# Transpositions of activations, norms and attention operands issued one at a time between split products instead of in runs

## The chip, the cores and the metric

The kernel runs on one core of one Trainium2 chip. The metric is device time in microseconds (us), the median of several executions. One execution is also profiled; its trace gives the start and the duration of every instruction on each engine: PE (TensorE, matmuls and transpositions), PEld (its weight loads), DVE (VectorE), ACT (ScalarE), POOL (GpSimd) and SP (SyncE, which here issues the DMAs). Each engine takes its own instructions in the order in which the program holds them.

## The reference

256 tokens of 1024 features pass through two blocks; every number is float32.

```python
def reference(x, ...):
    x = first_block(x, ...)    # h = rmsnorm(x); x += short_conv_mixer(h)   h = rmsnorm(x); x += swiglu(h)
                               # h = rmsnorm(x); x += mla_mixer(h)          h = rmsnorm(x); x += moe_swiglu(h)
    return second_block(x, mem_2, ...)

def mla_mixer(h, ...):         # 8 heads; queries and keys of 128 + 64 (rope) features
    down = h @ w_down
    c_q, c_kv = rmsnorm(down[..., :384]), rmsnorm(down[..., 384:640])
    q, kv = c_q @ w_uq, c_kv @ w_ukv
    q, k = rmsnorm(q), rmsnorm(k)          # then rope on 64 of the 192 features
    p = softmax(mask(q @ k.T * scale));  return (p @ v) @ w_o

def moe_swiglu(h, router, w_gate, w_up, w_down):   # 8 experts, the best two of each token
    gates = top_k(softmax(h @ router), 2)
    for e in range(8): out += gates[:, e] * swiglu(h, w_gate[e], w_up[e], w_down[e])

def second_block(x, mem, ...):
    z = rmsnorm(h) @ w_in                          # q, k, v of 8 heads of 64, pooling input, forget logits
    fox = forgetting_attention(q, k, v, f_logit)   # causal softmax with a decay
    pool = multiscale_pool(p_in, w_pool, pool_scale)   # trailing means of 4 groups, a linear map, a scale
    h += concat(fox, pool) @ w_out
    h += attention_to(mem) @ w_mem_out
    h += swiglu(rmsnorm(h))
```

## The kernel before

All work is in one program, written as steps. A string such as `MLA_ORDER` lists the steps of a stage; `play` appends them, and `run` calls them one after the other. The order in which steps are called is the order of the instructions in every engine's queue; nothing reorders them later. A step `f1` or `f2` only converts one or two more pieces of weights.

Products are **split products**: a float32 operand is held as a rounded high part (a cast on ACT) and the rest as a low part (a subtraction on DVE, `split_to`, L219 and L220), and `mm3` issues three matmuls, high by high, low by high, high by low (L225 to L227). Weights arrive by DMA as `raw`, are cast to `wh` on ACT and reduced to `wl` on DVE, some 1.0 and 1.2 us for each piece of 128x1024, all through the kernel. The matmuls of a product have 512, 384, 320 or 256 columns.

A **transposition** is a matmul with the identity (`ident`) of a 128x128 block. A helper issues a run of 2 to 4 of them into one bank of PSUM with the tag `t`, and then at once the instruction that empties the bank: a split (ACT cast, DVE subtraction) for norms and activations, a copy on ACT or DVE for attention operands. There are **two** banks of that tag, taken in turn; outputs of attention values, pooling products (`pooled`, `mapped`) and the experts' gather take them too. So a transposition or a product that opens such a bank waits until the last but one has been emptied.

Where transpositions stand: `Norm.turn(t)` (line L710 of `transposed`) transposes the rows of one of the two token tiles t after a norm, 8 of them, for the next stage; steps `zt` (t = 0) and `w` (t = 1). `Experts.turn` (L1236) transposes an expert's activations, 16 for each expert in four runs of four. In MLA, `turn` (L664) has the steps `R`, `K`, `Q` (rope part, key, query of a pair of heads, 4 each; R and K are emptied on ACT, Q on DVE, L666), and `causal_turn` (L552, step `y`) the three blocks of a softmax. In the forgetting attention (FOX) `turn` (L916) has `Q` (emptied on DVE) and `K` (on ACT, L918). In both, `s` are score products (L508, L509), `v` value products (L559, L560), `k` and `q` the products of keys and queries, `zp` products of the output projection, and in FOX `g` and `x` the pooling's two products; an `x` is scaled on ACT (L908) and split. After the last `zp` of a stage, the residual is added on DVE (L361), squared on ACT (L1147) and normed on DVE (L1160).

Of the kernel before, what the change touches and what calls it, by code (L numbers as in the profile page):

```python
# [68 lines left out]
FFN_HEAD = ("f1 f2 a00 f2 f1 a10 f2 f1 w a20 f1 f2 a21 a01 a30 f2 a31 f2 a11 f1 f2 f2 f2 f1 f1 f2 A u04 f2 f2 f2 "  # L69
    "f1 T f2 u05 f1 f1 f1 o0 o1 f2 f2 f2 f2 o2 f1 f2 f2 u06 f1 f2 u07 f1 f2 f1 f2 f1")  # L70
FFN_TAIL = ("f1 zp000 f2 zp010 zp001 zp011 zr00 zs00 f2 zp100 zr01 zs01 zp101 f2 zn0 zr10 f2 zp110 f1 zs10 zp111 "
    "zr11 zt zs11 zn1")
MLA_ORDER = ("b00 B a00 f2 w f2 p a10 a01 b01 c0 f2 f1 a11 f2 b10 c1 L0 b11 h0 L1 f2 h1 k00 l0 k01 f2 k10 l1 f2 "
# [5 lines left out]
ROUTE_ORDER = ("k00 f1 n0 w k01 r0 n1 k10 r1 R k11 K O S f2 f1 G0 f1 f2 G1 f1 B f2")  # L79
TAIL_ORDER = ("v00 d00 d01 d10 d20 d11 h0 d21 f2 c00 h1 c10 v01 c11 zs10 f1 f2 f2 f2 zs00 zs11 c01 zs01 zn0 f1 zn1 "  # L80
    "v10 f2 zt f2 f2 f2 f1 v11 V f2")
FOX_ORDER = ("w b a000 a010 S00 a001 a100 F0 f1 f2 U00 a011 S01 F1 a101 f2 U01 D a111 S11 a110 a201 a200 S10 a210 "
# [7 lines left out]
FFN2_HEAD = ("f2 f2 a00 a10 f2 f1 f2 w a20 f2 f1 a01 a21 a11 a30 a31 f1 f1 A f2 u04 f1 f2 f1 T f2 f2 u05 f2 f2 f1 "  # L90
# [3 lines left out]
class Chunk:  # L94
    """A chunk of weights in DRAM, and once it is on chip, its two float32r parts."""
# [22 lines left out]
class Body:  # L118
    def __init__(self, ctx, tc, t, out):
# [8 lines left out]
        self.steps = []  # L128

# [4 lines left out]
    def add(self, fn, *chunks, rate=None):  # L134
        """rate: pieces of chunks ahead at the step's start."""
        for c in chunks:
            if c.first is None:
                c.first = len(self.steps)
            c.last = len(self.steps)
        self.steps.append((fn, chunks, AHEAD[1] if rate is None else rate))  # L140

    def run(self):
        order = list(dict.fromkeys(c for _, chunks, _ in self.steps for c in chunks))
        at = {c: i for i, c in enumerate(order)}
        self.loaded = done = need = 0  # chunks; pieces of chunks; chunks

        def piece():
            """The next piece of a chunk into its parts."""
# [12 lines left out]
        def fill(n):  # L161
            """Up to n pieces of chunks ahead."""
# [7 lines left out]
        for s, (fn, chunks, rate) in enumerate(self.steps):  # L170
# [31 lines left out]
    def buf(self, tag, shape, dt=F32):  # L202
        """A working tile; TAGS says how many of its kind there are."""
# [3 lines left out]
    def split(self, src):  # L207
        """Both parts of [128, 256] or [128, 512], in a tile each or in one."""
# [21 lines left out]
    def row(self, name, n, tag=None):  # L230
        """A row of the parameter vector, on every partition."""
# [5 lines left out]
    def rstd(self, tag, ss, n, width):  # L237
        """(ss / width + eps) ** -0.5 of a few columns."""
# [7 lines left out]
    def setup(self, gain):  # L246
# [10 lines left out]
        # TensorE's clock rises with use: it starts before the first rows are there  # L257
# [4 lines left out]
    def constants(self):  # L262
# [5 lines left out]
        # causal mask of a diagonal block: 0 where key <= query  # L268
# [4 lines left out]
        # triu[j, t] = 1 where j <= t; striu: j < t  # L273
# [12 lines left out]
        # 1 / (t + 1) of the first frames  # L286
# [3 lines left out]
        # the narrow weights of the router and of the forget gates: high and low parts side by side  # L290
# [7 lines left out]
    def rope_tables(self):  # L298
# [23 lines left out]
        def wrap(dst, src):  # L322
            # into [-pi, pi]
# [44 lines left out]
    def entering(self, norm):  # L368
        """Steps of a norm of the residual stream."""
        return norm and {"zs": lambda t, n: (lambda: norm.stats(t, n),), "zn": lambda t: (lambda: norm.scale(t),),  # L370
                         "zt": lambda: (lambda: norm.turn(0),), "w": lambda: (lambda: norm.turn(1),)} or {}

    def project(self, acc, c, r, part, start):
        """acc[t, n] += part.T @ row r of the chunk."""
# [48 lines left out]
    def ffn(self, norm, gu0, gu, down, nxt, orders):  # L423
        """gu0: gate and up of the first 512 features, by rows of tokens; gu: of the others, by features."""
# [6 lines left out]
        def row_part(i, t):  # L431
            """Chunk i % 2 of gate (i < 2) or up: k-tiles 4 (i % 2)... ."""
# [1048 lines left out]
```

## Time and profile before

| | |
|---|---|
| time, median of 3 executions | 1384.9 us (1384.81 to 1385.75) |
| span of the profiled execution, first to last instruction | 1383.6 us |
| mean granted TensorE clock over the span | 0.988 |
| PE busy | 1337.0 us, 97% of the span |
| DVE busy | 1012.6 us, 73% |
| ACT busy | 814.8 us, 59% |
| PE matmuls | 7395 |

The profiled execution has no time of its own apart from its span; the median stands 1.3 us above it, which is what lies around the first and last instruction. Busy shares are averages over stages. Matmuls are pipelined and overlap in the records, so starts, not durations, tell what a matmul costs: the distance from one start to the next.

### The profile page before, as it was taken

How to read it: one execution, taken by the hardware profiler on the slowest of the kernel's cores; microseconds unless marked ns; L12 is line 12 of the kernel's file. 1: busy time of each engine (PE TensorE's matmuls, PEld its weight loads, DVE VectorE, ACT ScalarE, POOL GpSimd, SP SyncE). 2: the span in 40 equal slices, each digit the busy share in tenths (PEclk: the TensorE clock that was granted, in tenths of full speed). 3: DMA queues.
4: the chain of work that ended last, by engine and by line, in shares of the span. 5: the costliest groups of instructions: out<-in, count | busy, mean ns of one | idle time of the engine just before them, and what ended most of it. 6: DMA issues, size and time to landing. Idle time of an engine off the chain costs nothing.

```text
span 1383.6 us, 18935 instructions
## 1 busy us (share of the span) xinstructions
PE 1337.0 (97%) x7395; PEld 1152.1 (83%) x7395; DVE 1012.6 (73%) x1346; ACT 814.8 (59%) x1198; POOL 35.3 (3%) x70
## 2 busy tenths in 40 slices
PE   7999999999997999999999999999989888999998
PEld 7997999987776888888888888888868777899997
DVE  5866465558777898998989898989976566654554
ACT  4544454446655786867777777777755455634442
POOL 1000000001000000000000000000002000000000
PEclk9999999999999999999999999999999899999999
DMA  7545455435334999898989898989963332444441
GB/s 274 216 183 187 163 213 183 175 114 199 131 117 175 342 351 351 335 355 340 352 326 364 322 370 321 365 321 359 353 257 127 116 118 107 159 176 182 183 183 61
DMA packets 49328, 329.54 MB, mean 238 GB/s; under 512 B 6352, under 2 KB 7248, under 8 KB 11216
## 3 DMA queue, kind: packets, MB, share of 16 engines
q1 hardware_dynamic: 48672, 328.18, 63.9%
q8 instruction: 59, 0.97, 0.3%
q14 instruction: 37, 0.30, 0.1%
q10 hardware_dynamic: 560, 0.09, 0.0%
HBM read 327.20 MB, written 1.05 MB: 237 GB/s over the span
## 4 chain that ended last, share of the span: by engine, by line
PE 64%; DVE 3%; ACT 1%; issue 0%; POOL 0%; DVEq 0%; ACTq 0%; POOLq 0%
PE ps L225 19%; PE ps L227 19%; PE ps L226 19%; PE ps L1200 2%; PE ps L1236 1%; DVE wl L220 1%; PE ps L1246 0%; PE ps L1245 0%; PE ps L508 0%; PE ps L559 0%; DVE e L893 0%; PE ps L710 0%; DVE n L1160 0%; PE ps L1065 0%; ACT wh L219 0%
## 5 line engine op out<-in xcount | busy, mean ns | idle before, releaser
L220 DVE TENSOR_TENSOR wl<-raw,wh 128x1024 fp32r<-128x1024 f32 (+2 forms) x622 | 717.3, 1201 | 97.9 <-ACT wh L219 96.2
L219 ACT CAST wh<-raw 128x1024 fp32r<-128x1024 f32 (+2 forms) x622 | 611.3, 1035 | 125.6 <-PE ps L226 87.5
L225 PE MATMUL ps<-x,wh 128*128 128x256 f32 x800 | 228.1, 285 | 0.3 <-ACT e L889 0.2
L227 PE MATMUL ps<-x,wh 128*128 128x256 f32 x800 | 227.4, 284 | 0.0
L226 PE MATMUL ps<-x,wl 128*128 128x256 f32 x800 | 227.4, 284 | 0.0
L225 PE MATMUL ps<-wh,n 128*128 128x512 f32 x560 | 222.4, 397 | 0.0
L227 PE MATMUL ps<-wl,n 128*128 128x512 f32 x560 | 218.6, 390 | 0.0
L226 PE MATMUL ps<-wh,n 128*128 128x512 f32 x560 | 218.1, 389 | 0.0
L225 PE MATMUL ps<-wh,x 128*128 128x512 f32 (+2 forms) x448 | 175.4, 392 | 0.3 <-ACT x L219 0.2
L227 PE MATMUL ps<-wl,x 128*128 128x512 f32 (+2 forms) x448 | 173.2, 387 | 1.8 <-DVE wl L220 1.8
L226 PE MATMUL ps<-wh,x 128*128 128x512 f32 (+2 forms) x448 | 172.6, 385 | 1.1 <-DVE x L220 1.1
L225 PEld LDWEIGHTS ps<-x,wh 128*128 128x128 f32 x800 | 154.1, 193 | 2.0 <-DVE c L220 0.5
L226 PEld LDWEIGHTS ps<-x,wl 128*128 128x128 f32 x800 | 154.2, 193 | 0.8
L227 PEld LDWEIGHTS ps<-x,wh 128*128 128x128 f32 x800 | 154.1, 193 | 0.2 <-DVE x L220 0.2
L227 PEld LDWEIGHTS ps<-wl,n 128*128 128x128 f32 x560 | 105.1, 188 | 23.0
L226 PEld LDWEIGHTS ps<-wh,n 128*128 128x128 f32 x560 | 105.3, 188 | 20.9
L225 PEld LDWEIGHTS ps<-wh,n 128*128 128x128 f32 x560 | 105.2, 188 | 20.6
L227 PEld LDWEIGHTS ps<-wl,x 128*128 128x128 f32 x448 | 84.1, 188 | 20.2 <-DVE wl L220 3.6
L467 ACT ACTIVATE e<-ps 128x256 f32<-128x256 f32 x36 | 13.9, 385 | 144.8 <-PE ps L227 144.8
L226 PEld LDWEIGHTS ps<-wh,x 128*128 128x128 f32 x448 | 84.2, 188 | 17.7 <-DVE x L220 2.1
L225 PEld LDWEIGHTS ps<-wh,x 128*128 128x128 f32 x448 | 84.2, 188 | 16.0 <-ACT x L219 0.7
L468 DVE TENSOR_TENSOR e<-e,ps 128x256 f32<-128x256 f32 x36 | 15.2, 421 | 101.5 <-ACT e L467 101.5
(302 smaller groups left out, 1443.2 us busy)
## 6 DMA issues: line engine op xcount, KB each, us to landing
raw<-in_moe SPq DMA_DIRECT2D x192, 1024.0 KB, 5.3
raw<-in_ffn_gu SPq DMA_DIRECT2D x22, 1024.0 KB, 4.9
raw<-in_gu SPq DMA_DIRECT2D x22, 1024.0 KB, 4.8
raw<-in_conv_in SPq DMA_DIRECT2D x11, 1024.0 KB, 5.8
raw<-in_ffn_down SPq DMA_DIRECT2D x11, 1024.0 KB, 4.9
raw<-in_down SPq DMA_DIRECT2D x11, 1024.0 KB, 4.9
raw<-in_w_mem SPq DMA_DIRECT2D x6, 1024.0 KB, 4.9
raw<-in_w_in SPq DMA_DIRECT2D x6, 1024.0 KB, 6.3
```

The source lines that it names most:

```text
L219: self.nc.scalar.copy(hi, src)
L220: self.nc.vector.tensor_tensor(lo, src, hi.bitcast(F32), ALU.subtract)
L225: mm(ps, lhsT=a[0], rhs=b[0], start=start, stop=False)
L226: mm(ps, lhsT=a[1], rhs=b[0], start=False, stop=False)
L227: mm(ps, lhsT=a[0], rhs=b[1], start=False, stop=stop)
L467: nc.scalar.activation(sg, b[:, :S], AF.Silu)
L468: nc.vector.tensor_mul(h, sg, b[:, S:])
L1200: nc.tensor.matmul(o, lhsT=self.norm.h[t][:, (k0 + k) * P:(k0 + k + 1) * P], rhs=sel[:, t], start=t == 0, stop=t == NT - 1)
L1236: nc.tensor.transpose(ps[:, k * P:(k + 1) * P], h[n][:, k * P:(k + 1) * P], b.ident)
```

## The change

Transpositions are no longer issued where their step stands. `turning` makes one function for each, the last of which also empties the bank; `between` puts them in a list; `mm3` takes one from the list after each of its three matmuls; and `run` issues what is left in a run at the end of a step that took any. Score and value steps of both attentions first issue what is waiting. The norm's steps have a second form, `wd` and `zd`, which put the transpositions in the list; `wd` replaces `w` in the two swiglu stages, MLA, the routing and FOX, and `zd` with a place one product step earlier replaces `zt` at the end of the first swiglu.

```diff
-FFN_HEAD = ("f1 f2 a00 f2 f1 a10 f2 f1 w a20 ...
+FFN_HEAD = ("f1 f2 a00 f2 f1 a10 f2 f1 wd a20 ...
...
-FFN_TAIL = (... "zn0 zr10 f2 zp110 f1 zs10 zp111 zr11 zt zs11 zn1")
+FFN_TAIL = (... "zn0 zr10 f2 zp110 f1 zs10 zd zp111 zr11 zs11 zn1")
...
-ROUTE_ORDER = ("k00 f1 n0 w k01 r0 n1 ...
+ROUTE_ORDER = ("k00 f1 n0 wd k01 r0 n1 ...
...
+            self.took = False
             fn()
+            if self.took:
+                self.flush()
...
+    def between(self, fns, now=False):
+        self.waiting += fns
+        if now:
+            self.flush()
+
+    def flush(self):
+        while self.waiting:
+            self.waiting.pop(0)()
+
+    def turning(self, srcs, after):
+        bank = []
+        def one(i, src):
+            if not bank:
+                bank.append(self.bank("t"))
+            m = src.shape[-1]
+            self.nc.tensor.transpose(bank[0][:m, i * P:(i + 1) * P], src, self.ident)
+            if i == len(srcs) - 1:
+                after(bank[0])
+        return [lambda i=i, src=src: one(i, src) for i, src in enumerate(srcs)]
...
-        mm(ps, lhsT=a[0], rhs=b[0], start=start, stop=False)
-        mm(ps, lhsT=a[1], rhs=b[0], start=False, stop=False)
-        mm(ps, lhsT=a[0], rhs=b[1], start=False, stop=stop)
+        for i, (x, y) in enumerate(((0, 0), (1, 0), (0, 1))):
+            mm(ps, lhsT=a[x], rhs=b[y], start=start and i == 0, stop=stop and i == 2)
+            if self.waiting:
+                self.waiting.pop(0)()
+                self.took = True
...
-            b = self.bank("t")
-            for h in range(2):
-                for t in range(NT):
-                    nc.tensor.transpose(b[:W, h * S + t * P:h * S + (t + 1) * P], g["qk", i, t][:, 2 * hp + h], self.ident)
-            d = g["T", hp, i] = self.buf("w2", [P, 2, S])
-            (nc.scalar.copy if i else nc.vector.tensor_copy)(d[:W].rearrange("p h s -> p (h s)"), b[:W])
+            def after(b):
+                d = g["T", hp, i] = self.buf("w2", [P, 2, S])
+                (nc.scalar.copy if i else nc.vector.tensor_copy)(d[:W].rearrange("p h s -> p (h s)"), b[:W])
+            self.between(self.turning([g["qk", i, t][:, 2 * hp + h] for h in range(2) for t in range(NT)], after))
...
```

The other helpers (`turn` of MLA, `causal_turn`, `transposed`, the swiglu's rows, `Experts.turn`) change in the same way. No instruction is added or left out. The line numbers of the helpers shift: all moved transpositions are on L201, split products on L254, splits on L247 and L248, the copies of MLA's and FOX's operands on L690 and L942.

DVE, at the end of the first swiglu and the start of MLA, before and after. `x<-x,ps_1548` is the last residual addition, which the norm of the second token tile needs, and the two `x_206` rows are the low parts of the first tile's transposed norm.

```order
187 L361 TENSOR_TENSOR x<-x,ps_1544 128x512
188 L220 TENSOR_TENSOR wl_2920<-raw_2698,wh_2919 128x640
189 L361 TENSOR_TENSOR x<-x,ps_1548 128x512
190 L220 TENSOR_TENSOR x_206_2934<-ps_2935,x_205_2933 128x4x128
191 L220 TENSOR_TENSOR x_206_2934<-ps_2942,x_205_2933 128x4x128
```

```order
187 L391 TENSOR_TENSOR x<-x,ps_1544 128x512
188 L248 TENSOR_TENSOR wl_2920<-raw_2698,wh_2919 128x640
189 L248 TENSOR_TENSOR x_206_2927<-ps_2929,x_205_2926 128x4x128
190 L248 TENSOR_TENSOR x_206_2927<-ps_2940,x_205_2926 128x4x128
191 L391 TENSOR_TENSOR x<-x,ps_1548 128x512
```

The addition moved behind the two low parts.

DVE in MLA, around step `k21` (whose key gain is the L617 row on `ps_3424`), before and after. The `w_312` and `w_318` rows empty the bank of `Q0`; the four `e` rows rotate the rope part of the next pair.

```order
249 L617 TENSOR_TENSOR q_3376<-ps_3379,rowk_norm_2977 128x2x128
250 L666 COPY w_312_3411<-ps_3406 128x512
251 L721 TENSOR_TENSOR e_313_3413<-q_3333,cos 128x256
252 L722 TENSOR_TENSOR e_315_3415<-q_3333,sin 128x4x32
253 L723 TENSOR_TENSOR e_315_3415<-q_3333,sin 128x4x32
254 L724 TENSOR_TENSOR e_313_3413<-e_313_3413,e_315_3415 128x256
255 L220 TENSOR_TENSOR wl_3421<-raw_3237,wh_3420 128x512
256 L617 TENSOR_TENSOR q_3376<-ps_3424,rowk_norm_2977 128x2x128
```

```order
249 L644 TENSOR_TENSOR q_3376<-ps_3379,rowk_norm_2977 128x2x128
250 L748 TENSOR_TENSOR e_307_3392<-q_3333,cos 128x256
251 L749 TENSOR_TENSOR e_309_3394<-q_3333,sin 128x4x32
252 L750 TENSOR_TENSOR e_309_3394<-q_3333,sin 128x4x32
253 L751 TENSOR_TENSOR e_307_3392<-e_307_3392,e_309_3394 128x256
254 L248 TENSOR_TENSOR wl_3400<-raw_3237,wh_3399 128x512
255 L644 TENSOR_TENSOR q_3376<-ps_3403,rowk_norm_2977 128x2x128
256 L690 COPY w_318_3435<-ps_3430 128x512
```

The copy of `Q0` moved behind the rotation, a weight part and the gain.

ACT in FOX, around the steps `K2 x0 y00 K1 y01 x1`, before and after. The 66x512 copies empty the banks of `K2` and `K1`, the 128x384 copies those of `y00` and `y01`; an `e` row scales an `x` product and the `n` row behind it casts it.

```order
1492 L219 CAST w_3504_17435<-e_3502_17430 128x256
1493 L918 COPY w_3506_17443<-ps_17438 66x512
1494 L908 ACTIVATE e_3508_17449<-ps_17445,cols 128x256
1495 L219 CAST n_3490_17357<-e_3508_17449 128x256
1496 L554 COPY w_3510_17457<-ps_17453 128x384
1497 L219 CAST wh_17462<-raw_17162 128x1024
1498 L918 COPY w_3512_17471<-ps_17466 66x512
1499 L219 CAST wh_17462<-raw_17162 128x1024
1500 L219 CAST wh_17475<-raw_17249 128x1024
1501 L554 COPY w_3514_17485<-ps_17481 128x384
1502 L908 ACTIVATE e_3516_17491<-ps_17487,cols 128x256
```

```order
1492 L247 CAST w_3504_17435<-e_3502_17430 128x256
1493 L935 ACTIVATE e_3507_17446<-ps_17438,cols 128x256
1494 L247 CAST n_3490_17357<-e_3507_17446 128x256
1495 L942 COPY w_3508_17451<-ps_17440 66x512
1496 L247 CAST wh_17456<-raw_17162 128x1024 x2
1497 L247 CAST wh_17462<-raw_17249 128x1024
1498 L579 COPY w_3511_17476<-ps_17470 128x384
1499 L935 ACTIVATE e_3512_17478<-ps_17468,cols 128x256
1500 L247 CAST n_3490_17357<-e_3512_17478 128x256
1501 L942 COPY w_3514_17487<-ps_17482 66x512
1502 L579 COPY w_3516_17493<-ps_17489 128x384
```

The copy of `K1` (the second 66x512 row) moved from behind one weight cast to behind three, the copy of `y00` and both scaled products.

## Rows read from the trace of the kernel before

**Rows 1.** The page: busy us (share of the span) xinstructions of each engine.
```profile
PE 1337.0 (97%) x7395; PEld 1152.1 (83%) x7395; DVE 1012.6 (73%) x1346; ACT 814.8 (59%) x1198; POOL 35.3 (3%) x70
```

**Rows 2.** The page: the chain that ended last, share by engine.
```profile
PE 64%; DVE 3%; ACT 1%; issue 0%; POOL 0%; DVEq 0%; ACTq 0%; POOLq 0%
```

**Rows 3.** Waits of PE: waiting line, releaser: us in total, times, longest.
```profile
PE ps L1200 <- DVE sel L1189: 7.8, 1, 7.8
```

**Rows 4.** Timeline of PE in the experts: start, duration in us, line, operation, count.
```profile
465.15 0.39 PE L227 MATMUL ps<-wl,n 128*128 128x512 f32 x1
465.38 0.60 PE L1236 MATMUL ps<-ident,w 128*128 128x128 f32 x4
465.73 0.48 PE L225 MATMUL ps<-wh,n 128*128 128x512 f32 x1
466.05 0.39 PE L226 MATMUL ps<-wh,n 128*128 128x512 f32 x1
```

**Rows 5.** Groups by line and form: busy us, mean ns, then idle time before.
```profile
L1236 PE MATMUL ps<-ident,w 128*128 128x128 f32 x128 | 19.2, 272 | 0.0
```

**Rows 6.** Timeline of DVE, first swiglu to MLA.
```profile
300.34 0.69 DVE L361 TENSOR_TENSOR x<-x,ps 128x512 f32<-128x512 f32 x1
301.39 1.29 DVE L220 TENSOR_TENSOR x<-ps,x 128x512 fp32r<-128x512 f32 x2 [0.37 <-ACT x L219]
...
312.71 0.42 DVE L585 TENSOR_TENSOR q<-ps,rowkv_a 128x256 f32<-128x256 f32 x1 [3.60 <-DMA rowkv_a<-in_rows]
```

**Rows 7.** Timeline of ACT, first swiglu to MLA.
```profile
300.77 1.07 ACT L219 CAST x<-ps 128x512 fp32r<-128x512 f32 x2 [0.67 <-PE ps L710]
301.73 0.64 ACT L1147 ACTIVATE w<-x 128x512 f32<-128x512 f32 x1
```

**Rows 8.** Timeline of PE, MLA's first projections.
```profile
315.99 0.44 PE L227 MATMUL ps<-wl,x 128*128 128x384 f32 x1 [0.67 <-DVE wl L220]
```

**Rows 9.** Timeline of PE in MLA: `Q0`, then the first scores.
```profile
337.13 0.66 PE L664 MATMUL ps<-ident,q 128*128 128x128 f32 x4 [0.16 <-ACT w L666]
...
339.03 0.38 PE L508 MATMUL ps<-w,w 128*128 128x128 f32 x2
```

**Rows 10.** Timeline of ACT in MLA: the copies of `R0` and `K0`.
```profile
336.45 1.13 ACT L666 COPY w<-ps 128x512 f32<-128x512 f32 x2
```

**Rows 11.** Timeline of DVE in MLA around `k21`.
```profile
337.85 0.68 DVE L666 COPY w<-ps 128x512 f32<-128x512 f32 x1
338.44 0.42 DVE L721 TENSOR_TENSOR e<-q,cos 128x256 f32<-128x256 f32 x1
...
340.24 0.42 DVE L617 TENSOR_TENSOR q<-ps,rowk_norm 128x256 f32<-128x256 f32 x1
```

**Rows 12.** Timeline of DVE in the routing: both token tiles' first operation.
```profile
414.80 0.15 DVE L748 TENSOR_TENSOR rl<-rl,ps 128x8 f32<-128x8 f32 x1
...
418.10 0.16 DVE L748 TENSOR_TENSOR rl<-rl,ps 128x8 f32<-128x8 f32 x1 [0.32 <-ACT rl L747]
```

**Rows 13.** Timeline of PE in FOX: `y00`, then the scores `s11`.
```profile
1089.90 0.55 PE L552 MATMUL ps<-ident,w 128*128 128x128 f32 x3 [2.05 <-ACT w L918]
...
1093.32 0.63 PE L508 MATMUL ps<-w,w 66*128 66x128 f32 x2
```

**Rows 14.** Timeline of ACT in FOX: `K2`, a weight cast, `K1`.
```profile
1089.27 0.57 ACT L918 COPY w<-ps 66x512 f32<-66x512 f32 x1
...
1090.94 1.04 ACT L219 CAST wh<-raw 128x1024 fp32r<-128x1024 f32 x1
1091.88 0.58 ACT L918 COPY w<-ps 66x512 f32<-66x512 f32 x1
```

**Rows 15.** Timeline of PE in FOX: the scores `s30`.
```profile
1118.12 0.38 PE L508 MATMUL ps<-w,w 66*128 66x128 f32 x2
```

**Rows 16.** Timeline of ACT in FOX: scale of the product `x3`.
```profile
1118.12 0.48 ACT L908 ACTIVATE e<-ps,cols 128x256 f32<-128x256 f32 x1
```

**Rows 17.** Timeline of DVE in FOX: the copy of `Q3`.
```profile
1116.93 0.68 DVE L918 COPY w<-ps 66x512 f32<-66x512 f32 x1
```

More of the change, by code (lines that the diff above doesn't have):

```diff
@@ L451, in rows_turn @@
             for t in range(NT):
-                b = self.bank("t")
-                for k in range(4):
-                    nc.tensor.transpose(b[:, k * P:(k + 1) * P], rows["h"][t][:, k * P:(k + 1) * P], self.ident)
-                ts = slice(t * P, (t + 1) * P)
-                self.split_to(th[:, :, ts], tl[:, :, ts], b.rearrange("p (k m) -> p k m", m=P))
+                self.transposed(rows["h"][t], 4, th, tl, t, False)
             for k in range(4):
@@ L546, in causal_turn @@
     def causal_turn(self, d, h):
-        nc = self.nc
         p = d["p"][h]
-        b = self.bank("t")
-        for c in range(3):
-            nc.tensor.transpose(b[:, c * P:(c + 1) * P], p[:, c * P:(c + 1) * P], self.ident)
-        pT = d["pT", h] = self.buf("w2", [P, 384])
-        nc.scalar.copy(pT, b[:, :384])
+        def after(b):
+            pT = d["pT", h] = self.buf("w2", [P, 384])
+            self.nc.scalar.copy(pT, b[:, :384])
+        self.between(self.turning([p[:, c * P:(c + 1) * P] for c in range(3)], after))
     def causal_values(self, o, v, pT):
@@ L659, in turn, with after @@
             d = st[c]
-            b = self.bank("t")
-            for i in range(2):
-                for t in range(NT):
-                    src = d["rope"][i][:, t].rearrange("p h d -> p (h d)") if w == "r" else d[w][:, t, i, :NOPE]
-                    nc.tensor.transpose(b[:, i * S + t * P:i * S + (t + 1) * P], src, self.ident)
-            o = d[w + "T"] = self.buf("w2", [P, 2, S])
-            (nc.vector.tensor_copy if w == "q" else nc.scalar.copy)(o.rearrange("p h s -> p (h s)"), b)
+            def after(b):
+                o = d[w + "T"] = self.buf("w2", [P, 2, S])
+                (nc.vector.tensor_copy if w == "q" else nc.scalar.copy)(o.rearrange("p h s -> p (h s)"), b)
+            self.between(self.turning([d["rope"][i][:, t].rearrange("p h d -> p (h d)") if w == "r" else d[w][:, t, i, :NOPE]
+                                       for i in range(2) for t in range(NT)], after))
         def scores(c, h):
+            self.flush()
             d = st[c]
@@ L673, in values @@
         def values(c):
+            self.flush()
             d = st.pop(c)
@@ L704, in mla, with transposed @@
         self.play(MLA_ORDER, step)
-    def transposed(self, src, nk, xh, xl, t):
-        b = self.bank("t")
-        for k in range(nk):
-            self.nc.tensor.transpose(b[:, k * P:(k + 1) * P], src[:, k * P:(k + 1) * P], self.ident)
+    def transposed(self, src, nk, xh, xl, t, now=True):
         ts = slice(t * P, (t + 1) * P)
-        self.split_to(xh[:, :nk, ts], xl[:, :nk, ts], b[:, :nk * P].rearrange("p (k m) -> p k m", m=P))
+        self.between(self.turning([src[:, k * P:(k + 1) * P] for k in range(nk)], lambda b: self.split_to(
+            xh[:, :nk, ts], xl[:, :nk, ts], b[:, :nk * P].rearrange("p (k m) -> p k m", m=P))), now)
     def rope(self, dst, src, ts, nh):
@@ L1160, in scale, with turn @@
             nc.vector.scalar_tensor_tensor(h[:, s], self.rows(t)[:, s], r, self.g[:, s], op0=ALU.mult, op1=ALU.mult)
-    def turn(self, t):
-        b, nc = self.b, self.b.nc
+    def turn(self, t, now=True):
+        b = self.b
         if t == 0:
@@ L1230, in act, with turn @@
         return h
-    def turn(self, h, th, tl, k0, n):
-        b, nc = self.b, self.b.nc
-        ps = b.bank("t")
-        for k in range(4):
-            nc.tensor.transpose(ps[:, k * P:(k + 1) * P], h[n][:, k * P:(k + 1) * P], b.ident)
+    def turn(self, h, th, tl, k0, n, now=False):
+        b = self.b
         ks = slice(k0 + 4 * n, k0 + 4 * n + 4)
-        b.split_to(th[:, ks], tl[:, ks], ps.rearrange("p (k m) -> p k m", m=P))
+        b.between(b.turning([h[n][:, k * P:(k + 1) * P] for k in range(4)],
+                            lambda ps: b.split_to(th[:, ks], tl[:, ks], ps.rearrange("p (k m) -> p k m", m=P))), now)
     def combine(self, e, ys, back, t, n):
@@ L1338, in slow @@
                 for n in range(2):
-                    self.turn(h, th, tl, 8 * half, n)
+                    self.turn(h, th, tl, 8 * half, n, True)
             y = self.two()
```

35 lines of the change are left out of this document (19 added, 16 removed).

## The prediction

> **What bounds the kernel now.** I read the page first. PE is busy 97% of the span and carries most of the chain that ended last [rows 1, 2], so the first thought is that only what a transposition costs PE matters. But the share is an average: in the experts PE never waits, while between stages and inside the two attentions it stands still for a copy, a split or a chain on DVE; the longest single wait is for the routing [rows 3]. So I read two things: the timeline of PE where it is full, for the price of a transposition, and the timelines of ACT and DVE at the places where PE waits, for what happens when the emptying of a bank is issued later than before. The queue orders in the section on the change tell what stands behind what; the times come from the trace.
>
> **The price on PE, in a run and alone.** In a run of four among products of 512 columns [rows 4] the product ahead starts at 465.15, the first transposition 0.23 later (a product's normal pitch), the four are 0.11 apart, the next product starts 0.03 after the last of them, and the one behind that 0.32 later, not 0.23. From 465.15 to 466.05 are 0.90 us; two products take 0.46; so four transpositions cost 0.44, or 0.11 each. I read this so: each matmul needs its weights loaded first; a long product hides the load of what follows it, a transposition is too short to. In a run every transposition pays for the next one's load, and the last for the product's, seen as the late second product. Alone between products, the transposition's own load is hidden, the next product's is not: 0.23 + 0.03 + 0.32 is 0.58 for two products and one transposition, 0.12 for the transposition. Unrounded the difference to a run is about 7 ns. By the order, 181 transpositions now stand alone between two products, 124 of them among products of 512 columns (64 in the experts). 124 x 7 ns is 0.9 us; some fall into waits, so I take **+0.7**. The bound below: if a lone one cost only the 0.03 to the next start, each would save 0.08, and 181 of them 14.5 us.
>
> The Trainium skill (TensorE: Matmul & The Clock Gate, Architectural detail) says that PE's queue is a partial reorder window which can pull a weight load ahead of matmuls in flight, and that the queues of ACT and DVE are strictly first in, first out. The first half speaks for the saving of 14.5: with loads pulled far enough ahead a lone transposition would lie under the products. [Rows 4] do not show it: the product behind the run still comes 0.09 late, though it has four transpositions ahead of it in the queue. The second half is what the rest of the sum is made of.
>
> **The price of a later copy.** A bank is now emptied when its last transposition is issued, inside or behind a later step, so the emptying stands behind other work of ACT and DVE that the later step or a weight fill put there. Site by site:
>
> *First swiglu to MLA.* The last residual addition ran at 300.34, ahead of the first tile's low parts, which ended at 302.68 [rows 6]; the square of its row followed on ACT at 301.73 [rows 7]. Now the addition stands behind the low parts. They end no earlier: the eight transpositions and six products of `zp111` take PE as long in either order. So the addition ends at about 302.65 + 0.69 = 303.3, and the square, the norm of tile 1 and everything that SP issues behind it start 1.5 late. The row `rowkv_a` is one of these; DVE waited 3.60 for it until 312.71 [rows 6], the weight parts stand behind that on DVE, and PE waited for them at 315.99 [rows 8]. Nothing in that chain has slack: **+1.5** (if the first low part goes ahead early, 1.3). `wd` in MLA itself falls into this wait.
>
> *MLA, first pair.* `R0`, `K0`, `Q0` waited for `R0`'s copy and ran ahead of `k21` [rows 9, 10]; the copy of `Q0` was done at 338.53 [rows 11], under the products of `k21`, and the scores began at 339.03 without a wait [rows 9]. Now the copy stands behind the rotation, a weight part and the key gain. Without the copy ahead of them these come 0.6 earlier than in [rows 11]: the gain at 339.65, done at 340.0, the copy at 340.7. `Q0`'s transpositions are done before that. Scores at 340.7: **+1.6**. Behind them stand maximum, exponentials and the next copies in one chain. In two more places a bank is freed late, `R1`'s (by `Q1`'s copy, now behind a softmax's scaling) and `K2`'s (by `Q2`'s); from the lengths of those operations I estimate 0.4 and 0.5, **+0.9**. The other sites there have products enough behind them.
>
> *Routing.* The 8 transpositions of tile 1 come between the 12 products of `k01`, 0.34 apart, so the last starts at about 414.9, not 413.1; the cast (0.6) and the second low part (0.7) follow it and end at 416.2, where the pair had ended at 414.8. On DVE the router's chain of tile 0 stands behind it, at 414.80, and tile 1's chain began after a pause of only 0.32 [rows 12]. 1.4 - 0.3 is **+1.1**. This chain leads to `sel`, for which PE waits 7.8 us [rows 3], so all of it arrives.
>
> *Experts.* No transposition waited [rows 5]. The first half of each pair of runs is now emptied behind two weight casts, about 2 us later; the products that read it are two steps of twelve products away, over 5 us. Nothing beyond the 7 ns.
>
> *FOX.* (a) `K1`, two heads' keys. `K2`'s copy was at 1089.27 and `K1`'s at 1091.88, behind one weight cast of 1.04 [rows 14]; the scores `s11` started at 1093.32 [rows 13]. Now at 1089.27 the scale of `x0` and its cast go first, `K2`'s copy ends at about 1090.65 and `y00` starts at 1090.7, not 1089.90 [rows 13]. Behind that copy stand three weight casts (3.0), `y00`'s copy (0.4) and the scale of `x1` (0.5): 1094.4. `K1`'s bank is the one that `x1`'s scale frees, so its transpositions start there (0.8 for four, an estimate from PE's pitches there), its copy takes 0.6: `s11` at 1095.9, **+2.5**. (b) `Q3`. `x3` and `K3` now share a step, `Q3`'s bank is freed by the scale of `x3`, and that stands where it stood, behind four exponentials, at 1118.12 [rows 16]. `Q3`'s transpositions start at 1118.65, its copy (1116.93 before [rows 17]) comes behind a split of `x3` at 1119.5 and ends at 1120.2; `s30` starts there, not at 1118.12 [rows 15]: **+2.1**. (c) `Q2` waits for the low part of the first values, a wait that its run used to fill, and `y10` no longer fills the wait behind `g3`: estimates 0.6 and 0.2, **+0.8**. (d) At `a000` and `a211` one product goes ahead of a wait: **-0.4**.
>
> The attention to the memory and both swiglus up to their tails keep their ACT and DVE orders: 0.
>
> Sum: 0.7 + 1.5 + 1.6 + 0.9 + 1.1 + 2.5 + 2.1 + 0.8 - 0.4 = **+10.8 us**. The span of 1383.6 becomes 1394.4; with the 1.3 around it **1395.7**, against the median of 1384.9.
>
> **Rivals.** *Loads hidden (the other side).* A lone transposition lies under the products, 0.08 saved on each of 181: -14.5, with the late copies (10.1) 1380.5. It wins from 0.056 saved for each. For it: [rows 4] hold no lone one, so the reading is an inference. Against: the late product in those rows.
> *Copies absorbed.* ACT and DVE are busy only 59% and 73% [rows 1]; if other waits at the same places end last anyway, late copies cost nothing and 0.7 - 0.4 remains: 1385.2, no change. It needs all sites to have slack; [rows 6, 8, 9, 12] say that four have none.
> *More than the sum.* PE idles longer in the two attentions; where it has idled the granted clock has fallen in this trace, so the delays of FOX could bring some 5 us at the lower clock: 1400.7.
>
> **How the numbers follow.** The sum with parts absorbed or doubled: 0.80; hidden loads 0.08; absorbed 0.09; more than the sum 0.03. 0.2% is 2.8 us, about what a measurement of this kernel can tell from no change. Faster 0.08, same 0.09, slower 0.83. The range, 1386.5 to 1401, takes in half of the late copies absorbed (1390) and nearly all, and the extra clock loss; it leaves out the hidden loads and most of the fully absorbed case.
>
> **What will show it.** In the experts: products 0.23, a lone transposition 0.12 of extra pitch, no new wait. DVE: the addition at the end of the first swiglu behind two low parts. PE: a wait of about 1.6 before the first scores of MLA, for DVE's copy; before `s11` and `s30` waits for a copy. If a pair of product and transposition has a pitch well under 0.30, my reading of the loads is wrong; if PE reaches `s11` or `s30` without a wait, the FOX terms are.

## The result, and the profile after

The changed kernel takes **1404.6 us** (median of 4 executions, 1404.27 to 1404.99) against 1384.9 before: a ratio of 1.0141, 95% interval 1.0129 to 1.0154. The direction was right, the size was not: +19.7 us where +10.8 was forecast, and outside the range. The profiled execution has a span of 1402.7 us.

The page of the changed kernel, first part, answers to [rows 1]: the counts are equal, PE's busy time is 10.8 us longer, the other 8.3 us of the 19.1 by which the span grew are idle.

```profile
PE 1347.8 (96%) x7395; PEld 1156.4 (82%) x7395; DVE 1013.8 (72%) x1346; ACT 815.7 (58%) x1198; POOL 35.3 (3%) x70
```

A busy time that grows with no matmul added is a first hint: either each transposition costs more, or PE ran slower somewhere. Both traces hold the same 6911 matmuls that are not transpositions, in the same order. So I took the start of each in the changed kernel less its start before, and read where this shift grows (us, worked out from the two timelines):

| place | shift before it | behind it | grows by |
|---|---|---|---|
| end of the first swiglu to MLA's projections (315.99 before) | 0.0 | 1.2 | 1.2 |
| MLA, first scores `s00` (339.03) | 1.2 | 3.1 | 1.9 |
| MLA, `s00` to near the end of `q21` (347.45) | 3.1 | 7.3 | 4.2 |
| rest of MLA | 7.3 | 8.0 | 0.7 |
| routing, second tile's ranks (420.67) | 8.1 | 9.3 | 1.3 |
| all eight experts (435.9 to 1000.9) | 9.9 | 10.4 | 0.4 |
| FOX, to `s11` (1093.32) | 10.4 | 12.7 | 2.3 |
| FOX, `s11` to `s20` (1110.41) | 12.7 | 13.6 | 1.0 |
| FOX, to the product just ahead of `s30` (1118.00) | 13.6 | 16.1 | 2.4 |
| FOX, from there to the middle of `o0` (1122.29) | 16.1 | 20.2 | 4.1 |
| the rest | 20.2 | 19.1 | -1.1 |

The last row is no gain of the change. The kernel before has a spell there, a stretch with TensorE at half its clock, near 1169; the changed one has none behind the same wait of 2.06 us (more of this under what stays open).

Two steps of about 4 us begin at a place where a copy is late, but lie in matmuls that wait for nothing in this trace.

**The waits.** Timeline of DVE in the changed kernel at the end of the first swiglu; it answers to [rows 6].

```profile
302.34 0.69 DVE L248 TENSOR_TENSOR x<-ps,x 128x512 fp32r<-128x512 f32 x1 [0.21 <-ACT x L247]
302.95 0.68 DVE L391 TENSOR_TENSOR x<-x,ps 128x512 f32<-128x512 f32 x1
```

The addition stands behind the low part and ends at 303.6, where 303.3 was forecast. Timeline of DVE and then of PE in MLA (answers to [rows 11] and [rows 9]): the key gain, the copy of `Q0`, the first scores.

```profile
340.93 0.42 DVE L644 TENSOR_TENSOR q<-ps,rowk_norm 128x256 f32<-128x256 f32 x1
341.26 0.68 DVE L690 COPY w<-ps 128x512 f32<-128x512 f32 x1
```

```profile
338.21 1.28 PE L201 MATMUL ps<-ident,q 128*128 128x128 f32 x7
342.09 0.46 PE L535 MATMUL ps<-w,w 128*128 128x128 f32 x2 [2.61 <-DVE w L690]
...
346.25 1.17 PE L535 MATMUL ps<-w,w 128*128 128x256 f32 x2
```

PE had done its transpositions and waited 2.61 us for that copy. Timelines of ACT and PE in FOX around `K1` (answers to [rows 14] and [rows 13]): three weight casts, the copy of `y00`, the scale of `x1`, and the copy of `K1` only at 1105.35.

```profile
1100.40 0.57 ACT L942 COPY w<-ps 66x512 f32<-66x512 f32 x1
1100.88 2.94 ACT L247 CAST wh<-raw 128x1024 fp32r<-128x1024 f32 x3
1103.72 0.47 ACT L579 COPY w<-ps 128x384 f32<-128x384 f32 x1
1104.09 0.47 ACT L935 ACTIVATE e<-ps,cols 128x256 f32<-128x256 f32 x1
...
1105.35 0.58 ACT L942 COPY w<-ps 66x512 f32<-66x512 f32 x1 [0.35 <-PE ps L201]
```

```profile
1104.24 1.06 PE L201 MATMUL ps<-ident,q 128*66 128x128 f32 x4 [2.13 <-ACT w L579]
1105.10 0.85 PE L201 MATMUL ps<-ident,w 128*128 128x128 f32 x3
1105.98 0.80 PE L535 MATMUL ps<-w,w 66*128 66x128 f32 x2
```

And at `x3`, with the release of `Q3`'s bank and the copies behind it (answers to [rows 15] to [rows 17]):

```profile
1130.21 0.38 PE L201 MATMUL ps<-ident,q 128*66 128x128 f32 x2
1132.55 1.06 PE L201 MATMUL ps<-ident,q 128*66 128x128 f32 x4 [1.96 <-ACT e L935]
...
1134.40 0.79 PE L535 MATMUL ps<-w,w 66*128 66x128 f32 x2
```

**The clock.** Windows of the changed kernel: length, busy us of each engine, then the granted clock (1.00 is 2.4 GHz, 0.50 is 1.2 GHz), DMA share and GB/s.

```profile
336.00:340.00 4.00, 3.35 (x20) 2.37 (x18) 3.95 (x11) 4.00 (x16) 0.00 (x0) 1.00 0.58 203
340.00:342.00 2.00, 0.00 (x0) 0.00 (x0) 2.00 (x5) 0.57 (x2) 0.00 (x0) 1.00 0.81 311
342.00:344.00 2.00, 1.91 (x8) 1.37 (x9) 0.79 (x3) 0.00 (x0) 1.09 (x1) 0.90 0.55 201
344.00:346.00 2.00, 2.00 (x7) 1.07 (x6) 0.62 (x2) 0.00 (x0) 0.55 (x1) 0.50 0.90 352
350.00:352.00 2.00, 2.00 (x8) 1.85 (x8) 0.67 (x2) 1.99 (x5) 0.00 (x0) 0.50 0.00 0
354.00:356.00 2.00, 1.94 (x14) 1.69 (x13) 0.94 (x4) 1.01 (x2) 0.00 (x0) 1.00 0.00 0
1133.00:1137.00 4.00, 4.00 (x16) 3.06 (x15) 2.10 (x5) 1.30 (x3) 0.00 (x0) 0.50 0.00 0
1142.00:1146.00 4.00, 4.00 (x18) 3.25 (x18) 0.81 (x4) 0.00 (x0) 0.00 (x0) 0.96 0.77 266
```

The reader is to see the order: a stretch in which PE does nothing (0.00 busy from 340 to 342), then PE busy again from 342.09, still at full clock at first (0.90 over the window to 344), then at half clock for some 10 us without a gap, then full clock again. In FOX the clock falls at 1132.1, before the wait of 1.96 us behind `x3` ends. The kernel before in the windows that hold these scores:

```profile
341.00:345.00 4.00, 4.00 (x24) 3.07 (x24) 2.66 (x10) 0.68 (x1) 1.65 (x1) 1.00 0.80 289
1118.00:1122.00 4.00, 4.00 (x28) 3.43 (x27) 3.55 (x12) 3.94 (x9) 0.00 (x0) 1.00 0.00 0
```

Windows of 1 us each over both traces, each counted with twice what its clock lacks to 1, give the time at half clock without the first 20 us: 27 us before (near 428, 1032, 1090 and 1169) and 51 us after (near 343, 435, 1043, 1101 and 1132).

### The profile page after: what moved, and what is told of

Read it like the earlier page. It is cut to its first block, busy times and chain, and to the rows that moved or that the text cites. A ratio compares the mean times of both kernels' runs of the same rounds, so it can differ in the third digit from the quotient of the medians.

```text
span 1402.7 us, 18930 instructions
## 1 busy us (share of the span) xinstructions
PE 1347.8 (96%) x7395; PEld 1156.4 (82%) x7395; DVE 1013.8 (72%) x1346; ACT 815.7 (58%) x1198; POOL 35.3 (3%) x70
## 4 chain that ended last, share of the span: by engine, by line
PE 63%; DVE 3%; ACT 1%; issue 0%; DMA 0%; POOL 0%; SPq 0%; DVEq 0%; ACTq 0%; POOLq 0%
PE ps L254 56%; PE ps L1228 2%; PE ps L201 2%; DVE wl L248 1%; PE ps L535 1%; PE ps L1272 0%; PE ps L1271 0%; DMA rowg_q_fox<-in_rows 0%; ACT wh L247 0%; PE ps L586 0%; DVE n L1188 0%; DVE c L248 0%; ACT w L1078 0%; PE ps L1093 0%; ACT e L1046 0%
## 5 line engine op out<-in xcount | busy, mean ns | idle before, releaser
L248 DVE TENSOR_TENSOR wl<-raw,wh 128x1024 fp32r<-128x1024 f32 (+2 forms) x622 | 716.1, 1201 | 95.4 <-ACT wh L247 93.5
L247 ACT CAST wh<-raw 128x1024 fp32r<-128x1024 f32 (+2 forms) x622 | 611.3, 1035 | 134.9 <-PE ps L254 91.7
L254 PE MATMUL ps<-wh,n 128*128 128x512 f32 x1120 | 353.3, 396 | 0.0
L254 PE MATMUL ps<-x,wh 128*128 128x256 f32 x1600 | 296.4, 286 | 0.5 <-ACT e L916 0.5
L254 PE MATMUL ps<-wh,x 128*128 128x512 f32 (+2 forms) x896 | 280.6, 392 | 1.5 <-DVE x L248 1.5
L254 PEld LDWEIGHTS ps<-x,wh 128*128 128x128 f32 x1600 | 253.7, 194 | 2.1 <-ACT e L916 0.7
L254 PEld LDWEIGHTS ps<-wh,n 128*128 128x128 f32 x1120 | 208.5, 189 | 43.9 <-issue 0.6
L254 PE MATMUL ps<-x,wl 128*128 128x256 f32 x800 | 228.4, 286 | 0.0
L254 PE MATMUL ps<-wl,n 128*128 128x512 f32 x560 | 220.0, 393 | 0.0
L254 PEld LDWEIGHTS ps<-wh,x 128*128 128x128 f32 x896 | 166.5, 188 | 36.4 <-DVE x L248 2.9
L254 PE MATMUL ps<-wl,x 128*128 128x512 f32 (+2 forms) x448 | 175.2, 391 | 2.6 <-DVE wl L248 2.6
L254 PEld LDWEIGHTS ps<-x,wl 128*128 128x128 f32 x800 | 154.8, 193 | 0.8
L254 PEld LDWEIGHTS ps<-wl,n 128*128 128x128 f32 x560 | 105.5, 188 | 23.1 <-issue 0.2
L254 PE MATMUL ps<-wh,w 128*128 128x512 f32 x352 | 111.1, 396 | 0.0
L254 PEld LDWEIGHTS ps<-wl,x 128*128 128x128 f32 x448 | 84.1, 188 | 21.7 <-DVE wl L248 5.0
L254 PEld LDWEIGHTS ps<-wh,w 128*128 128x128 f32 x352 | 65.1, 188 | 14.6
L254 PE MATMUL ps<-wl,w 128*128 128x512 f32 x176 | 69.8, 396 | 0.0
L247 ACT CAST x<-ps 128x512 fp32r<-128x512 f32 x64 | 37.1, 585 | 51.7 <-PE ps L201 49.8
L248 DVE TENSOR_TENSOR x<-ps,x 128x512 fp32r<-128x512 f32 x64 | 43.3, 688 | 13.2 <-ACT x L247 12.7
L247 ACT CAST w<-e 128x256 fp32r<-128x256 f32 x48 | 19.5, 407 | 52.8 <-DVE e L440 26.6
```

Of the source, the lines that this page charges most:

```text
L247: self.nc.scalar.copy(hi, src)
L248: self.nc.vector.tensor_tensor(lo, src, hi.bitcast(F32), ALU.subtract)
L254: mm(ps, lhsT=a[x], rhs=b[y], start=start and i == 0, stop=stop and i == 2)
```

## The experiments

Theory A: copies and splits stand later in the queues of ACT and DVE, PE waits for them, and a longer wait is followed by a stretch at half clock which costs PE a second time. Theory B, the rival: the loss lies in the lone transpositions between products themselves, in their price on PE or in a clock that they let fall. In all runs below, the times are medians, measured beside the kernel before (medians of 1384.5 to 1385.2 in these). The changed kernel was not run again beside them, so differences to its 1404.6 carry that drift of up to 0.4 us. Shifts are those of a run's one profiled execution.

**1. MLA's first pair in runs at once (mla0_now).**

```diff
-            self.between(self.turning([d["rope"][i]... for t in range(NT)], after))
+            self.between(self.turning([d["rope"][i]... for t in range(NT)], after), c == 0)
```

> The changed kernel, but the three operands of MLA's first pair (R0, K0, Q0) are transposed in runs at once, as before. Theory A (late copies make PE wait, and a wait near 2.5 us lets the granted clock fall to half for some 10 us): the wait before the first scores (1.9 us) and the half clock behind it (about 4.0 us) both go, 1404.6 - 5.9 = 1398.7 us, and the granted clock stays 1.0 from the first scores to the second pair's. Theory B (lone transpositions between products lower PE's pace or clock by themselves, all over the kernel): only 6 of 181 lone ones go, 1404.4 us.

Measured: 1399.8 us (1399.16 to 1400.23), ratio 1.0109 (1.0092 to 1.0126). From 1404.6 that is 4.8 less for 6 lone transpositions; in the trace no half clock is left between the first scores and the second pair. Theory A holds. By the shift, the 1.1 it misses has two parts: between `s00` and 347.45 the shift still grows by 1.1 at full clock (why, under 3 and 4), and a short spell at half clock near 308 us, in MLA's projections, which this profile has and that of the changed kernel has not, leaves 0.5.

**2. K3 and Q3 in runs at once (fox3_now).** The same edit in FOX's `turn`, with `hp == 3`.

> The changed kernel, but K3 and Q3 of the forgetting attention are transposed in runs at once, as before. Theory A: the wait ahead of the scores s30 (2.4 us) and the half clock behind it (about 4.1 us) go, 1404.6 - 6.5 = 1398.1 us. Theory B: 3 of 181 lone ones go, 1404.5 us.

Measured: 1400.4 us (1397.19 to 1401.68), ratio 1.0106 (1.0089 to 1.0123): 4.2 less. The spell behind `s30` is gone from the trace, and from `s20` to the middle of `o0` the shift grows by 0.3 where it grew by 6.5: at the place itself theory A is right in size too. What is missing lies elsewhere. The profiled execution (1401.7, the slowest of the four) has the spell near 308, a longer one in MLA (342 to 356, where the changed kernel had 343 to 354) and one near 1185, in stretches that the edit does not touch. How long PE stays at half clock differs from execution to execution of this one kernel too: its fastest, of 1397.2 us, had a mean granted clock of 0.984, this one 0.979.

**3 and 4. The waits kept, and filled (fill_products, fill_transposes).** Work for PE that no one reads, ahead of the first scores in MLA and behind `x3` in FOX; the transposed variant:

```diff
         def scores(c, h):
             self.flush()
+            if c == 0 and h == 0:
+                fb = self.bank()
+                for i in range(22):
+                    nc.tensor.transpose(fb[:, i % 4 * P:(i % 4 + 1) * P], self.ident, self.ident)
...
             self.mm3(ob, cpool[q * P:(q + 1) * P], g.pop(("m", q)), True, True)
+            if q == 3:
+                fb = self.bank()
+                for i in range(18):
+                    nc.tensor.transpose(fb[:, i % 4 * P:(i % 4 + 1) * P], self.ident, self.ident)
```

> The changed kernel with idle work added for PE: 22 products of 256 columns ahead of MLA's first scores and 18 behind the product x3, each set into a bank that nothing reads. The copies stay as late as they are. Theory A: the two waits are as long as before, but the clock stays at 1.0, and 4.0 + 4.1 us come back: 1396.5 us. Theory B: the clock or the pace is set by the lone transpositions and not by the two waits: 1404.6 us or a little more.

> The same two fillings with transpositions of the identity in place of the products (22 and 18). Theory A, with a transposition as good as a product for the clock: 1396.5 us. Theory A, with transpositions not counted as activity, as the Trainium skill (TensorE: Matmul & The Clock Gate, Part 4) says of them: the clock falls as without them, 1404.6 us. Theory B: 1404.6 us.

Measured: 1397.7 us with products (ratio 1.0100, 1.0080 to 1.0119) and 1397.4 with transpositions (1.0094, 1.0077 to 1.0111): 7 us back for added work. Timeline of PE in the kernel with transpositions:

```profile
339.48 2.56 PE L700 MATMUL ps<-ident 128*128 128x128 f32 x22
342.24 0.46 PE L535 MATMUL ps<-w,w 128*128 128x128 f32 x2 [0.19 <-DVE w L690]
```

The scores start at 342.24 as late as without the filling (342.09), for the same copy. Its windows there:

```profile
342.00:350.00 8.00, 7.81 (x43) 5.67 (x42) 3.36 (x12) 2.37 (x6) 1.64 (x1) 1.00 0.50 178
1131.00:1139.00 8.00, 8.00 (x44) 6.56 (x45) 5.19 (x13) 5.25 (x14) 0.00 (x0) 1.00 0.23 69
```

The same window of the changed kernel:

```profile
342.00:350.00 8.00, 7.91 (x25) 4.82 (x26) 2.55 (x10) 0.27 (x1) 1.65 (x1) 0.60 0.45 176
```

With the filling the clock is 1.00 behind both waits, and from 342 to 350 PE gets through 43 matmuls where it did 25. The delay is the copy's, most of the stretch behind it is the clock's, and it is PE's idleness that lets the clock fall; all 181 lone transpositions are still there. Theory B falls.

How much is the clock's, the shift tells. With transpositions as filling it still grows by 1.2 from `s00` to 347.45 and by 0.3 from 1118.00 to 1122.29, against 4.2 and 4.1. The 1.2 is a wait that PE at half clock came too late to meet, for the bank of `R1`, which the copy of `Q1` frees:

```profile
351.44 0.33 PE L201 MATMUL ps<-ident,e 128*128 128x128 f32 x1 [1.34 <-DVE w L690]
```

So the two prices do not add up: where the half clock goes, another late copy shows. Half clock behind the two waits cost some 7 us net, not 8.3.

On the clock, transpositions do as well as products here. The Trainium skill (TensorE: Matmul & The Clock Gate, Part 4) says that transpositions do not count as activity in the same way; these transpositions of float32 by the identity held the clock, and the measurement decides for this form. Whether they run in the mode that the page means, the trace does not tell.

**5. The experts alone (experts_only).** The kernel before, and of the change only `Experts.turn`.

> The kernel before with the change in the experts alone: 64 of their 128 transpositions stand alone between products, everything else is issued in runs at its old place. Theory A (a lone transposition costs PE 7 ns more than one in a run, the rest of the loss is late copies and clock): 1384.6 + 0.5 = 1385.1 us. Theory B (the loss lies in the lone transpositions themselves): 64/181 of 19.7, 1391.6 us. The rival of the prediction (weight loads hidden under products): 64 x 0.084 less, 1379.2 us.

Measured: 1385.5 us (ratio 1.0004, 0.9995 to 1.0013): no change that can be told, and 64 lone transpositions are no gain. In its profile the shift grows by 0.3 over the eight experts. Timeline of PE in the changed kernel, the run that answers to [rows 4]:

```profile
475.41 0.39 PE L254 MATMUL ps<-wh,n 128*128 128x512 f32 x1
475.64 0.27 PE L201 MATMUL ps<-ident,w 128*128 128x128 f32 x1
475.66 0.49 PE L254 MATMUL ps<-wh,n 128*128 128x512 f32 x1
475.99 0.27 PE L201 MATMUL ps<-ident,w 128*128 128x128 f32 x1
...
476.71 0.48 PE L254 MATMUL ps<-wh,n 128*128 128x512 f32 x1
477.02 0.40 PE L254 MATMUL ps<-wl,n 128*128 128x512 f32 x1
```

From 475.41 to 477.02 are 1.61 us for five product pitches (5 x 0.227, as 12 products in a row have) and four transpositions: 0.12 each, as forecast. The reason that the prediction gives for it, which weight loads are hidden, was not varied by any run.

**6. Both attentions in runs at once (attention_now).** `now` is true in `turn` of MLA and FOX and in `causal_turn`; norms, activations and experts keep the change.

> The changed kernel, but all operands and softmax blocks of MLA and of the forgetting attention are transposed in runs at once, as before; norms, activations and experts keep the change. Theory A: what the norms' late splits cost stays (end of the first swiglu 1.2, routing some 1.9, experts 0.6): 1388.3 us, with no half clock in MLA and none behind s20. Theory B: 118 or so of 181 lone ones stay, 1397 us.

Measured: 1388.9 us (ratio 1.0032, 1.0020 to 1.0044). So 4.2 of the loss are the norms and experts, and some 15.5 the operands of attention.

**7 to 9. Three more terms undone, one at a time (fox1_now, route_now, tail_now).** `hp == 1` as in 2; `w` in place of `wd` in the routing; `zt` at its old place.

> The changed kernel, but K1 and Q1 of the forgetting attention are transposed in runs at once, as before. Theory A (late copies, then the clock): the scores s11 come 2.4 us earlier, and the spell at half clock around them is 3.4 us shorter, worth about 1.5: 1404.6 - 3.9 = 1400.7 us. Theory B (the loss lies in lone transpositions): Q1 and K1 were issued in runs in the changed kernel too, so 1404.6 us.

> The changed kernel with w in place of wd in the routing: the norm's eight transpositions in a run ahead of k01. Theory A: the router's chain on DVE starts earlier by what the prediction gave it, 1.1 us, or by the 1.5 to 2 us that the trace of the changed kernel shows at the ranks: 1403 us. Theory B: 8 of 181 lone ones go, 1403.7 us.

> The changed kernel with zt at its old place at the end of the first swiglu: the last residual addition stands ahead of the low parts again. Theory A: 1.5 us by the prediction, 1.2 by the trace of the changed kernel: 1403.3 us. Theory B: 6 of 181 lone ones go, 1403.9 us.

Measured: 1402.0 us (1399.94 to 1403.08), 1402.8 (1402.38 to 1404.82) and 1401.5 (1399.56 to 1402.78), 2.6, 1.8 and 3.2 less than 1404.6; ratios 1.0123, 1.0131 and 1.0113, intervals some 0.0015 to either side. The routing is where A put it: the shift at the ranks stays at 7.8, where it rose by 1.3. The tail gives back more than the copy's 1.2. In its profile the spell at half clock at the start of the experts is 3.4 us shorter too, which by the shift is worth 0.3 there (in the profile of the routing the same spell is shorter too, worth 0.9). That profiled execution is only 1.8 us faster than the changed kernel's; where the median of 3.2 comes from stays open. For `K1` the forecast of 1400.7 lies within the interval, by a little. In its profile the spell around `s11` did get 3.4 us shorter, and the shift from 1080 to `s20` grows by 0.7 where it grew by 3.3, so 2.6 of the forecast 3.9. That profile, the fastest of its four, also has a spell of only 3.4 us behind `x3`, where the others have 10.2, after much the same wait (1.90 us). The times do not tell A from B for the routing and the tail; for `K1`, where B has nothing to remove, time and trace speak for A.

**10. The kernel before with its own waits filled (before_fill).** Transpositions as in 4, as a step of their own at four places.

```diff
-ROUTE_ORDER = ("k00 f1 n0 w k01 r0 n1 k10 r1 R k11 K O S f2 f1 G0 ...
+ROUTE_ORDER = ("k00 f1 n0 w k01 r0 n1 k10 r1 R k11 K O S f2 f1 I64 G0 ...
...
-    "v10 f2 zt ...                K2 x0 y00 ...                d00 s10 e01 ...
+    "v10 f2 I30 zt ...            K2 x0 I18 y00 ...            d00 I18 s10 e01 ...
```

> The kernel before with idle work for PE in its four longest waits: transpositions of the identity into a bank that nothing reads, 64 ahead of the experts' first gather, 30 ahead of the last norm's transposition after the experts, 18 behind the pooling's first mapped product, 18 ahead of the memory's second scores. Nothing else moves. If a wait costs a second time through the clock behind it: the spells at half clock from 428, 1032, 1090 and 1169 go, and where PE is the bound in them half of their length comes back, about 2 + 1.5 + 4.5 + 1, so 1375.5 us. If the half clock there costs nothing because other engines bound these stretches: 1384.5 us.

Measured: 1388.9 us (ratio 1.0029, 1.0018 to 1.0041), a miss. Timeline of its PE at the routing:

```profile
431.20 9.72 PE L194 MATMUL ps<-ident 128*128 128x128 f32 x64 [7.24 <-DVEq L791]
440.76 0.50 PE L1207 MATMUL ps<-sel,c 128*128 128x128 f32 x3
```

I had put the filling behind a branch on a count that PE reads and waits for: the wait was at the branch, not at the gather, so 64 transpositions ran after it, the first 5 us of them at half clock, and put the gather 9.2 late. Of the three other places two gave something back, 4.0 us in all: the shift falls by 2.4 in FOX (4.5 expected; a spell of 3.4 us remains, near 1105) and by 1.5 at the memory's scores (1 expected). Ahead of the last norm after the experts the spell near 1032 is gone and nothing comes back (1.5 expected): there the half clock had cost nothing that the shift shows.

**11. Another order in FOX (early_scores).** The kernel before; scores that need no pooling fill the wait for the pooling's sums.

```diff
-    e0 d00 g0 g1 K2 x0 y00 d01 f1 K1 f2 y01 x1 s11 s10 m1 v0
+    e0 d00 K1 g0 K2 g1 s11 s10 x0 y00 d01 f1 f2 y01 x1 m1 v0
```

> The kernel before with another order of steps in the forgetting attention: K1 is transposed ahead of g0, K2 ahead of g1, and the scores s11 and s10 come right behind g1, in the time in which PE waited for the pooling's sums. Theory A: the waits of 2.05 and 0.63 us shrink by some 2 us and the clock does not fall behind them, some 4 more: 1378.5 us. If the late copies and waits there are not what sets the time: 1384.5 us.

Measured: 1382.8 us (ratio 0.9986, 0.9977 to 0.9995), faster than both kernels, by 2.0 and 21.8 us, though by less than forecast. Its timeline of PE:

```profile
1088.88 0.49 PE L552 MATMUL ps<-ident,w 128*128 128x128 f32 x3
1091.40 0.61 PE L552 MATMUL ps<-ident,w 128*128 128x128 f32 x3 [2.02 <-DVE w L544]
...
1094.04 1.22 PE L559 MATMUL ps<-w,n 128*128 128x256 f32 x2 [1.69 <-ACT w L554]
```

The wait of [rows 13] has moved from the bank of `K2` to `d01` on DVE, and the clock still falls, from 1093 to 1103. By the shift, only 0.8 of the 3.3 us that this profile gains lie in FOX. Another 1.5 lie at the memory's scores, which the edit does not touch: the spell near 1169 is missing there, behind the same wait of 2.05 us. So the gain is measured, but the order in FOX is shown as the cause of less than half of it.

**12. Both ideas together (tuned).** `d01` early too, `y00 y01` ahead of `x0 x1`, and three fillings, that of the routing ahead of the branch.

```diff
-    e0 d00 g0 g1 K2 x0 y00 d01 f1 K1 f2 y01 x1 s11 s10 m1 v0
+    e0 d00 d01 K1 g0 K2 g1 s11 s10 y00 y01 x0 x1 f1 f2 m1 v0
-    K O S f2    v10 f2 zt    d00 s10
+    K I60 O S f2    v10 f2 I30 zt    d00 I18 s10
```

> The kernel before, with no transposition moved between products, in the order that the two findings point to: in the forgetting attention K1 and d01 ahead of g0, K2 ahead of g1, then s11, s10, y00, y01, and only then x0 and x1; and idle transpositions for PE in three waits (60 ahead of the routing's branch, 30 ahead of the last norm after the experts, 18 ahead of the memory's second scores). Theory A: the waits around y00 and y01 go with the half clock behind them (4.5 us), and the other three spells shrink (1.6 + 0.6 + 1.3): 1376.7 us. If half clock costs nothing in these places: 1381 us.

Measured: 1386.3 us (ratio 1.0009, 1.0000 to 1.0018), a miss. The order took the waits away up to the first values; then PE stood still, by its timelines of PE and DVE:

```profile
1093.92 0.39 PE L567 MATMUL ps<-w,n 128*128 128x128 f32 x2
1100.50 0.79 PE L566 MATMUL ps<-w,n 128*128 128x256 f32 x1 [6.19 <-DVE c L227]
```

```profile
1095.56 3.50 DVE L227 TENSOR_TENSOR wl<-raw,wh 128x1024 fp32r<-128x1024 f32 x3 [0.52 <-ACT wh L226]
1098.97 1.15 DVE L527 TENSOR_REDUCE sm<-ps 128x1 f32<-128x128 f32 x4
1100.04 0.41 DVE L227 TENSOR_TENSOR c<-ps,c 64x256 fp32r<-64x256 f32 x1
```

The split that frees the values' bank stands behind three weight parts and four maxima; in the old order the weight parts ran while PE was at the scores. It is the study's own lesson once more: the price of an order is paid by a copy that it puts behind something else. Of the three fillings only the memory's paid, 1.5 by the shift. The one ahead of the branch kept the clock at 1.00 through the routing, though PE still waited 2.59 us for `sel` behind it, and made the kernel no faster (0.3 later in the experts). Behind the one ahead of the last norm after the experts the shift grew by 1.6.

## Why the prediction was right in kind and wrong in size

**The price of a lone transposition** was right: 0.12 against 0.11 in a run; 64 of them moved the time by less than can be told. Its reason, the weight loads, stays a reading. The rival of hidden loads is out: at 0.08 saved on each, experiment 5 would have been at 1379.2.

**The late copies** were right, place by place. Forecast and growth of the shift: end of the swiglu 1.5 and 1.2; `Q0` 1.6 and 1.9; routing 1.1 and 1.3; `K1` 2.5 and 2.3; `Q3` 2.1 and 2.4. In sum 8.8 was forecast and 9.1 came; the rival that they are absorbed is out. One term was too small: for the banks of `R1` and `K2` 0.9 was forecast, and with the clock kept (fill_transposes) the shift grows by 2.0 in MLA behind `s00`.

**What failed is the step from the copies to the sum.** It was made as if PE, once released, ran at the pace of the trace before: the half clock behind the new waits stands in the sum with nothing. Two of the waits that it foresaw left PE idle so long that the granted clock went from 2.4 to 1.2 GHz, and the stretches behind them, in which PE then waited for nothing, took 4.2 and 4.1 us more. Filling just these waits gave 7 of the missing 8.9 us back (1397.4 and 1397.7, inside the range); the rest of the 8.3 stays even so, as the wait for `R1`'s bank above all. The mechanism was written down as the third rival, with 5 us and a chance of 0.03, for FOX alone. The evidence for more stood in the trace of the kernel before: it has a spell at half clock behind each of its four longest waits (near 428, 1032, 1090 and 1169), and the forecast delays of 1.6 and 2.1 were joined to idle time that was there already in shorter waits (0.20, 0.26 and 0.16 from `R0` to `Q0`; 0.48 ahead of `Q3` and 0.80 ahead of `x2`): 2.61 and, with a first wait of 0.8 just ahead, 1.96 in the end. I had read these spells only as a feature of FOX.

**What stays open**: when a wait makes the clock fall. Waits of 1.06, 0.48 and 0.80 within 5 us were harmless before. And the same wait can go either way. Ahead of the memory's second scores PE waits 2.05 or 2.06 us in twelve of the profiles here; a spell of 3.4 us at half clock follows in six of them and none in the other six. The wait and a window behind it, in the kernel before and then in the changed one:

```profile
1167.63 1.13 PE L1032 MATMUL ps<-mk,n 128*128 128x256 f32 x4 [2.06 <-DVE n L1027]
1169.00:1172.00 3.00, 3.00 (x10) 2.47 (x11) 1.58 (x6) 0.95 (x3) 0.00 (x0) 0.52 0.00 0
```

```profile
1187.87 1.13 PE L1060 MATMUL ps<-mk,n 128*128 128x256 f32 x4 [2.06 <-DVE n L1055]
1188.00:1192.00 4.00, 3.75 (x24) 3.04 (x25) 2.93 (x9) 2.87 (x9) 0.00 (x0) 1.00 0.01 2
```

In MLA the wait of some 2.6 us was followed by a spell in all five profiles that have it unfilled, while the wait of 2.59 us behind the filling in experiment 12 was not. Executions of the kernel before alone had mean clocks from 0.984 to 0.988, at 1386.5 and 1384.3 us. So part of the size of a loss like this can be chance. I can say that filling or avoiding those two waits keeps the clock, and not where the limit lies.

## What to carry to other kernels

A change that spreads a run of work among other work moves not only that work but also what empties its result; look in the order of every other engine at what now stands ahead of the copy, before looking at the price on the engine that was to gain. On TensorE, price a new wait of the length seen here (2.61 us, or 1.96 behind one of 0.80) twice: once as idle time, and once as matmuls at half clock behind it, some 3 to 4 us here. And where such a wait can't be avoided, cheap matmuls that no one reads can be worth their instructions, but try each place by itself: they gave 7 us back in the changed kernel's two waits, some in FOX and at the memory's scores, and nothing at the routing or ahead of the last norm after the experts. Behind a branch that the engine waits at, they only add to the wait.

## What the runs showed of the hardware that was not expected

22 and 18 float32 transpositions by the identity, run in two waits, kept the granted clock at 1.00 where without them it was 0.50 for some 10 us each; as many products did the same (1397.4 us with transpositions, 1397.7 with products). The same wait of 2.05 or 2.06 us was followed by 3.4 us at half clock in six profiles and by none in six. And PE's wait for a value that steers a branch held up all that stood behind it: 64 transpositions issued behind the branch began only at 431.20, after 7.24 us of waiting.
